# An output projection and a feed-forward's opening as one written sequence, with weights split ahead; a recurrent layer entered before its root

## The chip, the cores and the metric

The kernel runs on one NeuronCore of one Trainium2 chip. The metric is the device time of one execution in microseconds (us), lower is better. Engines are called as the profile calls them: PE is TensorE's matmul, PEld its weight loads, DVE is VectorE, ACT is ScalarE, POOL is GpSimd, SP is SyncE, which here only issues DMAs.

## The reference, cut to what matters

One inference step with two trunk layers over 512 latent and 128 context tokens of width 1024, all in f32. Layer 0 mixes tokens by attention, layer 1 by a gated linear recurrent unit (LRU); each is followed by a SwiGLU feed-forward of inner width 2816. The parts that the change touches:

```python
def _modulate(x, g, shift, scale):            # ahead of each sub-layer
    return _rms_norm(x, g) * (1 + scale[:, None, :]) + shift[:, None, :]

def _swiglu(x, w_gu, w_down):
    gate, up = jnp.split(x @ w_gu, 2, axis=-1)
    return (jax.nn.silu(gate) * up) @ w_down

def _lru_mixer(xm, h0, w_in, conv_w, conv_b, w_a, b_a, w_i, b_i, lam, w_out):
    gate, xr = jnp.split(xm @ w_in, 2, axis=-1)
    xc = _centred_depthwise_conv(xr, conv_w, conv_b).astype(jnp.float32)
    ...                                        # coefficients, two scans: hs_f, hs_b
    y = (hs_f + hs_b).astype(xm.dtype) * jax.nn.gelu(gate)
    return y @ w_out, jnp.stack([hT_f, hT_b], axis=1)

        lat = lat + g1_l[:, None, :] * o_l     # residual behind the mixer
        f_l = _swiglu(_modulate(lat, norm_g[i, 1], sh2_l, sc2_l), ffn_w_gu[i], ffn_w_down[i])
        lat = lat + g2_l[:, None, :] * f_l
```

## The kernel before

Activations lie transposed: features on the 128 partitions (8 tiles of 128, index k or f), the 640 tokens along the free axis. f32 precision comes from splitting every operand into a high part `hi` (a cast to fp32r on ACT, L1217) and a low part `lo` (a difference on DVE, L1218; both in `split`). A product is three matmuls per 128 inputs: hi·hi, hi·lo, lo·hi. `chunk` (L227 and on, matmuls L233 to L235) makes 128 outputs for half of the tokens: 8 × 3 = 24 matmuls of 320 columns. `part` (L242 to L244) does the same for some of the k.

`unit` fetches one weight tile of 1024 × 128 and splits it, or, when its name is in `kept`, loads both parts ready made. `keep` makes these ready parts ahead of time: in the first feed-forward's second and third groups (`ffn`), two units an iteration, POOL loads raw weights into `kraw` (one buffer), ACT casts, DVE subtracts into `kw` (one buffer), POOL stores to DRAM (L197 to L203). Before the change that covers the LRU's 16 input units ("wi") and 8 output units ("wlo").

The order of instructions on each engine is made by a scheduler that works from a model of the durations, except where `in_order` (L1221 and on) fixes it: within its block the instructions of PE, DVE and ACT keep the order of the code. Tiles of a pool lie in memory in the order of their first use, and a pool opened later lies over the memory of those closed before it; a tile there waits for the tiles under it.

The RMS norm's factor per token, the root, is made by `stat` (L449 and on): matmuls of the sum of squares `ssq` and of the last square with a column of ones (L456, "at"), mean plus epsilon on DVE (L459), power −1/2 on POOL (L469), a diagonal matrix on DVE (L471), and a matmul of ones with it that spreads the factor over the partitions (L474, "rr" or "mx"). ACT copies it to `r` (L493 or L860).

The places that the change touches:

- **End of the first feed-forward.** `project` (its down projection) adds residuals (L499), squares, sums `ssq`, and scales x into the LRU's input `hi`, `lo`, without the root. Then `stats` makes the root for both token halves. Only then comes `lru`, in written order on PE, DVE and ACT: per unit f the input half `xa`, `xb`, `e1`, `e2` (L1087, times the root), convolution `c1`, `cv` (L1105, L1109), four gate products (L1118), tanh, exponentials and the scans, and the gate half `ga`, `gb`.
- **Output projection of the LRU.** `project_halves` does three output tiles with both token halves in six banks, with the last input tile last, and then the five others (`DEH`) in two passes over the halves; each residual's x is stored to the DRAM copy `xd` by SP (L836). After each half `stat` makes its root.
- **Opening of the second feed-forward.** `normed`, `first_half` and `second_half` multiply x by gain and root (L804), add the bias on ACT (L805) and split; the blocks are called B11 (first four k, first token half), B21, B12 and B22. `plain` makes hidden units 0 and 1 (`PLAIN` = 2) by ordinary products (L960 to L962). All further hidden units use a seven-product scheme over sums of blocks: `sums` makes T1 to T4 of the blocks (L824 to L827, the last on POOL) and splits them, and reloads x from `xd` for the later residuals; `sum_weights` makes S1 to S4 of the weights (L882) and splits them; `product` (L903 to L905) is called by `pair_a`, `pair_b` and `pair_c`.

Only two short stretches of this projection and opening are in written order before the change; the rest is placed by the scheduler, with `held` to keep some products behind the root's matmuls.

## Time and profile before

| | |
|---|---|
| device time, three executions | 1544.09, 1548.87, 1553.25 us; median 1548.87 |
| profiled execution | 1547.74 us, its span 1546.0 us |
| mean granted clock of TensorE | 0.985 |
| busy share PE / DVE / ACT / POOL | 97% / 70% / 46% / 16% |
| DMA | 238.60 MB moved, 154 GB/s on average |

The span runs from the first to the last instruction; all places in the trace are in us from its start. The first feed-forward's last down projection ends near 855, the LRU runs from there to about 1034, the output projection to about 1077, and the second feed-forward to the end. A line of the trace gives start, duration, engine, code line, operation, written tile and read tiles; "x12" merges twelve in a row, and the bracket is idle time before it with what ended it. A matmul's listed duration overlaps with the next one's, so its cost is the distance of starts. PEclk is the clock that TensorE was granted, as a share of the full one.

### The profile page before, as it was taken

Reading aid. Unit: us, or ns where it says so; the run is one execution under the profiler, and the core shown is the slowest. Engines: PE = TensorE matmul, PEld = TensorE weight load, DVE = VectorE, ACT = ScalarE, POOL = GpSimd, SP = SyncE. Lnnn points to the kernel's source line nnn. Section 1 sums busy time; section 2 is a strip of 40 time slices with the busy share of each in tenths; the row PEclk is TensorE's granted clock in tenths of the full one; section 3 lists DMA queues with packets and bytes.
Section 4 is the critical chain, followed back from the end, with each engine's and each line's share of the span. In section 5 each row is a group of like instructions: output and inputs, shape, how many; then the busy total and the mean of one; then the engine's idle time right before and its main releaser. Section 6 shows DMA issues by size and latency. Waiting matters only on the chain.

```text
span 1546.0 us, 26176 instructions
## 1 busy us (share of the span) xinstructions
PE 1492.1 (97%) x10311; PEld 1446.1 (94%) x10311; DVE 1078.2 (70%) x2040; ACT 713.9 (46%) x1312; POOL 251.6 (16%) x298
## 2 busy tenths in 40 slices
PE   6999999989999999999999999998999999999997
PEld 3899999889999999999999899988999999999997
DVE  5678788969899998555556278884776656565646
ACT  4676666664333123423434377763534343434242
POOL 2111122100111111110110011110132322222210
PEclk9999999999999999999999999999899999999998
DMA  9545556445556668666675533244232231323211
GB/s 378 160 114 167 168 161 183 146 140 192 170 195 187 202 207 276 213 236 229 229 234 175 195 129 123 69 173 161 63 117 82 81 107 58 100 65 99 66 55 68
DMA packets 80011, 238.60 MB, mean 154 GB/s; under 512 B 8816, under 2 KB 24336, under 8 KB 76688
## 3 DMA queue, kind: packets, MB, share of 16 engines
q1 hardware_dynamic: 61136, 157.07, 31.7%
q0 software_dynamic: 18464, 79.71, 16.1%
q8 instruction: 81, 1.33, 0.3%
q14 instruction: 42, 0.34, 0.1%
q10 hardware_dynamic: 288, 0.16, 0.0%
HBM read 196.26 MB, written 34.09 MB: 149 GB/s over the span
## 4 chain that ended last, share of the span: by engine, by line
PE 87%; DVE 6%; DMA 3%; ACT 2%; issue 1%; POOL 0%; SPq 0%; POOLq 0%; DVEq 0%; ACTq 0%
PE mm L233 14%; PE mm L234 14%; PE mm L235 14%; PE mx L235 5%; PE mx L233 5%; PE mx L234 5%; PE mx L903 3%; PE mx L904 3%; PE mx L905 3%; PE gp L1118 2%; PE op L739 2%; PE tp L663 1%; PE mc L903 1%; PE mc L904 1%; PE mc L905 1%; PE mm L257 1%
## 5 line engine op out<-in xcount | busy, mean ns | idle before, releaser
L233 PE MATMUL mm<-big,whi 128*128 128x320 f32 (+3 forms) x1011 | 313.6, 312 | 2.7 <-ACT whi L1217 1.6
L234 PE MATMUL mm<-big,whi 128*128 128x320 f32 (+3 forms) x1011 | 315.0, 312 | 1.2 <-DVE big L1218 1.2
L235 PE MATMUL mm<-big,wlo 128*128 128x320 f32 (+3 forms) x1011 | 314.1, 311 | 0.0
L271 DVE SCALAR_TENSOR_TENSOR mprod<-mraw,csb 128x1024 f32<-128x1024 f32 x160 | 195.5, 1222 | 5.6 <-DMA mraw<-in_wm 5.3
L233 PEld LDWEIGHTS mm<-big,whi 128*128 128x128 f32 x1011 | 190.8, 189 | 4.9 <-ACT whi L1217 1.9
L234 PEld LDWEIGHTS mm<-big,whi 128*128 128x128 f32 x1011 | 191.6, 190 | 2.7 <-DVE big L1218 1.9
L235 PEld LDWEIGHTS mm<-big,wlo 128*128 128x128 f32 x1011 | 191.7, 190 | 1.1
L1217 ACT CAST whi<-raw 128x1024 fp32r<-128x1024 f32 (+2 forms) x110 | 112.6, 1024 | 160.5 <-PE mm L234 105.9
L1218 DVE TENSOR_TENSOR wlo<-raw,whi 128x1024 fp32r<-128x1024 f32 (+2 forms) x110 | 136.3, 1239 | 38.3 <-ACT whi L1217 35.9
L235 PE MATMUL mm<-big,wlx 128*128 128x320 f32 (+3 forms) x498 | 154.7, 311 | 1.9 <-DMA wlx<-kwlo 1.9
L233 PE MATMUL mm<-big,whx 128*128 128x320 f32 (+3 forms) x498 | 154.6, 311 | 0.0
L234 PE MATMUL mm<-big,whx 128*128 128x320 f32 (+3 forms) x498 | 154.6, 310 | 0.0
L499 DVE SCALAR_TENSOR_TENSOR x<-mm,G,x 128x192 f32<-128x192 f32 (+3 forms) x207 | 83.5, 435 | 88.8 <-PE mm L235 88.4
L235 PE MATMUL mx<-big,wlo 128*128 128x320 f32 (+3 forms) x365 | 115.1, 315 | 1.0 <-DMA wlo<-kwlo 1.0
L233 PE MATMUL mx<-big,whi 128*128 128x320 f32 (+3 forms) x365 | 116.0, 318 | 0.0
L234 PE MATMUL mx<-big,whi 128*128 128x320 f32 (+3 forms) x365 | 114.6, 314 | 0.0
L267 POOL DMA_DIRECT2D mraw<-in_wm x80 | 43.2, 540 | 376.5 <-DVE mprod L271 265.3
L235 PEld LDWEIGHTS mm<-big,wlx 128*128 128x128 f32 x498 | 94.2, 189 | 2.1 <-DMA wlx<-kwlo 2.1
L234 PEld LDWEIGHTS mm<-big,whx 128*128 128x128 f32 x498 | 94.3, 189 | 0.0
L233 PEld LDWEIGHTS mm<-big,whx 128*128 128x128 f32 x498 | 94.1, 189 | 0.0
L1217 ACT CAST whx<-raw 128x1024 fp32r<-128x1024 f32 (+1 forms) x38 | 39.0, 1026 | 73.3 <-PE mm L234 42.2
L235 PEld LDWEIGHTS mx<-big,wlo 128*128 128x128 f32 x365 | 70.4, 193 | 1.5 <-DMA wlo<-kwlo 1.5
(332 smaller groups left out, 3719.7 us busy)
## 6 DMA issues: line engine op xcount, KB each, us to landing
raw<-in_gu SPq DMA_DIRECT2D x88, 512.0 KB, 3.6
mraw<-in_wm POOLq DMA_DIRECT2D x80, 512.0 KB, 3.9
kwi<-kw POOLq DMA_DIRECT2D x16, 1024.0 KB, 5.2
raw<-in_dn SPq DMA_DIRECT2D x24, 512.0 KB, 3.6
sw<-in_wm SPq DMA_DIRECT2D x16, 512.0 KB, 10.1
raw<-in_wqk SPq DMA_DIRECT2D x16, 512.0 KB, 4.4
kraw<-in_wi POOLq DMA_DIRECT2D x16, 512.0 KB, 6.1
kwlo<-kw POOLq DMA_DIRECT2D x8, 1024.0 KB, 5.2
```

The costliest lines, as they stand in the source:

```text
L233: nc.tensor.matmul(ps, hi[:, k], xhi[:, k, s], start=(k == 0), stop=False)
L234: nc.tensor.matmul(ps, hi[:, k], xlo[:, k, s], start=False, stop=False)
L235: nc.tensor.matmul(ps, lo[:, k], xhi[:, k, s], start=False, stop=(k == nk - 1))
L267: nc.gpsimd.dma_start(w, self.i["wm"][l * 6 + j - 2, f])
L271: nc.vector.scalar_tensor_tensor(prod, w, 1.0, self.csb[:, s], ALU.mult, ALU.mult, accum_out=out[:, s, f:f + 1])
L499: last = self.nc.vector.scalar_tensor_tensor(xs, ps[:, a - t0:b - t0], G[:, s, f:f + 1], xs, ALU.mult, ALU.add).ins
L739: mm = nc.tensor.matmul(out, v, w, start=start, stop=stop)
L903: nc.tensor.matmul(ps, hi[:, k], xh[:, k], start=start and k == 0, stop=False, skip_group_check=not start)
L904: nc.tensor.matmul(ps, hi[:, k], xl[:, k], start=False, stop=False, skip_group_check=not start)
L905: nc.tensor.matmul(ps, lo[:, k], xh[:, k], start=False, stop=(k == KH - 1), skip_group_check=not start)
L1217: self.nc.scalar.copy(hi, v)
L1218: return self.nc.vector.tensor_tensor(lo, v, hi.bitcast(F32), ALU.subtract).ins
```

## The change

It makes four edits.

1. `keep` also splits five units of the second feed-forward's gate and up weights (gate and up of hidden units 0 and 1, and the gate of unit 2), three units instead of two in each group's last iteration.
2. `stat` is cut into `root`, `diag` and `spread`. At the end of the first feed-forward `stats` is replaced by `entry`: seven eighths of the LRU's first product, then the root's matmuls over all 640 tokens at once (the last square is added to `ssq` on DVE), then the last eighth. The diagonal, the product of the other token half, the spread and the copies follow in `whole`, a new step of the LRU's written order.
3. `project_halves`, `plain` and the first lines of `ffn_halves` become one function, `opening`, wholly in written order on PE, DVE and ACT. In it `xd` is stored by POOL instead of SP, all weights of units 0 and 1 come ready split, T4 is made on DVE, the first S1 to S4 stand at fixed places, and x is reloaded after the weights of six units are asked for. The second root's and first root's matmuls, diagonal and spread stand inside other chunks.
4. The weight tiles of the opening's pool are first used ahead of the others, and the LRU's gate tile `gl` ahead of its input tiles, so the memory order of both pools is another.

The diff, cut to its core:

```diff
-            nc.gpsimd.dma_start(raw, self.i[name][f])
+            nc.gpsimd.dma_start(raw, self.i[name][1, f] if name == "gu" else self.i[name][f])
...
-        if k < KT - 1:
+        if k < KT - 1 or self.whole:
             nc.vector.tensor_tensor(self.ssq[:, s], self.ssq[:, s], q, ALU.add)
         self.lastq[t0] = [q]
...
+    def root(self, bl, parts, newton=False):
+        nc, n = self.nc, len(bl)
         ps = self.ps()
-        parts = [(self.ssq, 0)] + [(q, t0) for q in self.lastq.get(t0, ())]
...
+    def entry(self, hi, lo):
+        self.u0, self.p0 = self.unit(("wi", KT), "m"), self.pg(False)
+        t0, t1 = CHB[0]
+        ps = self.p0[:, 0:t1 - t0]
+        with self.in_order(ORDERED[:1]):
+            self.part(ps, self.u0, hi, lo, range(KT - 1), t0, t1)
+            self.rs = self.root(range(0, NTOK, P), [(self.ssq, 0)])
+            self.part(ps, self.u0, hi, lo, (KT - 1,), t0, t1)
...
-        if nxt:
+        if entry:
+            self.shift(*nxt)
+            self.entry(*nxt[1:])
+        elif nxt:
             self.stats()
             self.shift(*nxt)
...
         todo = [("wi", KT), ("wi", 0)] + [("wi", f + g) for f in range(1, KT) for g in (KT, 0)] + [("wlo", f) for f in range(KT)]
+        todo += [("gu", c * NF + f) for f in range(PLAIN) for c in range(2)] + [("gu", PLAIN)]
...
                 if ci:
-                    self.keep(todo, 2)
+                    self.keep(todo, 3 if j == n - 1 else 2)
...
+    def opening(self, w, hi, lo, gk, key, xd, l):
+        nc = self.nc
+        G = self.need(self.gcols, gk)
+        us = [self.unit(w[f], "m" if f < KT - DEH else "x") for f in range(KT - 2)]
+        self.load_x(xd)
+        banks = [(f, c, (self.ps("mx") if c else self.pg(False))[:, 0:HT]) for f in range(KT - DEH) for c in range(2)]
+        self.ssq = self.t([P, NTOK], F32, "ssq", 1, self.sb)
+        self.lastq, qs, hid, tmp = {}, {}, {}, {}
+
+        def mm(f, c, ks=range(KT), ps=None):
+            ps = self.pg()[:, 0:HT] if ps is None else ps
+            self.part(ps, us[f], hi, lo, ks, *CH[c])
+            return ps
+
+        def res(f, c, ps):
+            t0, t1 = CH[c]
+            self.residual(f, t0, t1, ps, G, False)
+            qs[f, c] = q = self.ssq[:, t0:t1] if f == 0 else self.t([P, HT], F32, "sq", 2, self.sb)
+            nc.scalar.activation(q, self.x[:, f, t0:t1], AF.Square)
+            nc.gpsimd.dma_start(xd[f * P:f * P + P, t0:t1], self.x[:, f, t0:t1])
+            if f == KT - 1:
+                self.lastq[t0] = [q]
+
+        def add(f, c):
+            t0, t1 = CH[c]
+            if 0 < f < KT - 1:
+                nc.vector.tensor_tensor(self.ssq[:, t0:t1], self.ssq[:, t0:t1], qs[f, c], ALU.add)
+
+        def start(s):
+            self.stat_spread(s)
+            nc.scalar.copy(self.rt[:, s[0]:s[1]], self.r[0][:, 0:s[1] - s[0]])
+
+        def halves(k, c):
+            n = f"B{1 + k // KH}{1 + c}"
+            return [self.X[n + p][:, k % KH] for p in "hl"]
+
+        def gain(k, c):
+            for s, a, b in _pieces(*CH[c]):
+                v = self.x[:, k, a:b]
+                nc.vector.scalar_tensor_tensor(v, v, A[:, s, k:k + 1], self.rt[:, a:b], ALU.mult, ALU.mult)
+            for s, a, b in _pieces(*CH[c]):
+                v = self.x[:, k, a:b]
+                nc.scalar.activation(v, v, AF.Identity, bias=B[:, s, k:k + 1])
+            nc.scalar.copy(halves(k, c)[0], self.x[:, k, slice(*CH[c])])
+
+        def low(k, c):
+            h, v = halves(k, c)
+            nc.vector.tensor_tensor(v, self.x[:, k, slice(*CH[c])], h.bitcast(F32), ALU.subtract)
+
+        def plain(u, c, ks=range(KT), ps=None):
+            ps = self.pg(False)[:, 0:HT] if ps is None else ps
+            for k in ks:
+                xh, xl = halves(k, c)
+                nc.tensor.matmul(ps, u[0][:, k], xh, start=(k == 0), stop=False)
+                nc.tensor.matmul(ps, u[0][:, k], xl, start=False, stop=False)
+                nc.tensor.matmul(ps, u[1][:, k], xh, start=False, stop=(k == KT - 1))
+            return ps
+
+        def gate(j, ps):
+            hid[j] = self.t([P, HT], F32, "g", 3, self.sb)
+            nc.scalar.activation(hid[j], ps, AF.Silu)
+
+        def outs(j, c):
+            return [t[:, j, c * HT:c * HT + HT] for t in (self.hhi, self.hlo)]
+
+        def up(j, c, ps):
+            nc.vector.tensor_tensor(hid[j], ps, hid[j], ALU.mult)
+            nc.scalar.copy(outs(j, c)[0], hid[j])
+
+        def rest(j, c):
+            nc.vector.tensor_tensor(outs(j, c)[1], hid[j], outs(j, c)[0].bitcast(F32), ALU.subtract)
+
+        def sums(k):
+            b11, b12, b21, b22 = [self.x[:, j, a:a + HT] for j in (k, k + KH) for a in (0, HT)]
+            t2 = self.t([P, HT], F32, "c22", 2, self.sb)
+            tmp[k] = ("T1", b11), ("T2", t2), ("T3", b12), ("T4", b21)
+            for n, v in zip(("T1", "T2", "T3", "T4"), ((b11, b12, b11), (t2, b22, b11), (b12, b22, b12), (b21, b21, t2))):
+                nc.vector.tensor_tensor(*v, ALU.subtract)
+                nc.scalar.copy(self.X[n + "h"][:, k], v[0])
+
+        def lows(k):
+            for n, v in tmp[k]:
+                nc.vector.tensor_tensor(self.X[n + "l"][:, k], v, self.X[n + "h"][:, k].bitcast(F32), ALU.subtract)
+            for j in (k, k + KH):
+                nc.sync.dma_start(self.x[:, j], xd[j * P:j * P + P])
+
+        last = KT - 1
+        self.blocks(self.t([P, 2 * KH, HT], F32R, "xt", 1, self.sb), ("T4h", "T4l"))
+        with self.in_order():
+            for ks in (range(KT - 2), (KT - 2,), (KT - 1,)):
+                for f, c, ps in banks:
+                    mm(f, c, ks, ps)
+            us += [self.unit(w[f], "m") for f in (KT - 2, KT - 1)]
+            f = KT - DEH
+            ps = mm(f, 0)
+            for i, (g, c, bank) in enumerate(banks):
+                res(g, c, bank)
+                if i:
+                    add(*banks[i - 1][:2])
+            res(f, 0, ps)
+            add(*banks[-1][:2])
+            add(f, 0)
+            for f in range(f + 1, KT):
+                res(f, 0, mm(f, 0))
+                add(f, 0)
+            f = KT - DEH
+            ps = mm(f, 1, range(KH))
+            st = self.stat_root(*CH[0])
+            mm(f, 1, range(KH, KT), ps)
+            st = self.stat_diag(st)
+            res(f, 1, ps)
+            add(f, 1)
+            f += 1
+            ps = mm(f, 1, range(KH))
+            start(st)
+            mm(f, 1, range(KH, KT), ps)
+            gain(0, 0)
+            gain(1, 0)
+            self.hhi, self.hlo = [self.big(n=NTOK + 2) for _ in range(2)]
+            for t, n in ((self.hhi, "T2"), (self.hlo, "T3")):
+                self.blocks(t, (n + "h", n + "l"))
+                h = t.rearrange("p k t -> p (k t)")[:, 2 * (NTOK + 2):2 * (NTOK + 2) + HB]
+                self.X["B12h" if n == "T2" else "B12l"] = h.rearrange("p (k t) -> p k t", k=KH)
+            self.hhi, self.hlo = [t[:, :, 0:NTOK] for t in (self.hhi, self.hlo)]
+            g0 = self.unit(("gu", 0), "m")
+            u0 = self.unit(("gu", NF), "x")
+            raw = self.t([P, KT, P], F32, "raw", 3)
+            nc.sync.dma_start(raw, self.i["gu"][l, PLAIN])
+            q = {"g": raw, "u": self.i["gu"][l, NF + PLAIN]}
+            for f in range(f, last):
+                k = 2 * (f - KT + DEH)
+                res(f, 1, ps)
+                ps = mm(f + 1, 1)
+                gain(k, 0)
+                low(k - 2, 0)
+                gain(k + 1, 0)
+                low(k - 1, 0)
+                add(f, 1)
+            low(KT - 2, 0)
+            low(KT - 1, 0)
+            res(last, 1, ps)
+            g1, u1 = self.unit(("gu", 1), "m"), self.unit(("gu", NF + 1), "m")
+            hi2, lo2 = self.unit(("gu", PLAIN), "x")
+            q["W"] = {n: (hi2[:, a:a + KH], lo2[:, a:a + KH]) for n, a in (("A11", 0), ("A12", KH))}
+            ps = plain(g0, 0, range(KH))
+            st = self.stat_root(*CH[1])
+            plain(g0, 0, range(KH, KT), ps)
+            gate(0, ps)
+            s12, s34 = self.s_sums(q)
+            s12(True)
+            st = self.stat_diag(st)
+            s34(True)
+            self.s_split(q, 0)
+            ps = plain(u0, 0, range(KH))
+            start(st)
+            plain(u0, 0, range(KH, KT), ps)
+            gain(0, 1)
+            up(0, 0, ps)
+            gate(1, plain(g1, 0))
+            gain(1, 1)
+            low(0, 1)
+            rest(0, 0)
+            for k in range(2, 6):
+                gain(k, 1)
+                low(k - 1, 1)
+            ps = plain(u1, 0)
+            up(1, 0, ps)
+            gain(6, 1)
+            low(5, 1)
+            rest(1, 0)
+            self.pair_a(q, False)
+            gain(7, 1)
+            low(6, 1)
+            low(7, 1)
+            sums(0)
+            q["g1"] = self.total(*q["g1"], "g")
+            lows(0)
+            sums(1)
+            gate(0, plain(g0, 1))
+            lows(1)
+            ps = plain(u0, 1)
+            sums(2)
+            up(0, 1, ps)
+            lows(2)
+            rest(0, 1)
+            gate(1, plain(g1, 1))
+            sums(3)
+            self.s_split(q, 1)
+            lows(3)
+            self.last_weights(q)
+            up(1, 1, plain(u1, 1))
+            rest(1, 1)
+        return q
...
+    def s_sums(self, q):
+        nc, g = self.nc, q["g"]
         q["u"], src = self.t([P, KT, P], F32, "raw", 3), q["u"]
         nc.sync.dma_start(q["u"], src)
+        ss = q["S"] = [self.t([P, KT, P], F32, "sum", 2, self.sb) for _ in range(2)]
         s1, s2, s3, s4 = [s[:, a:a + KH] for s in ss for a in (0, KH)]
         g1, g2, u1, u2 = [t[:, a:a + KH] for t in (g, q["u"]) for a in (0, KH)]
+        ops = (s1, u1, u2, ALU.add), (s2, s1, g1, ALU.subtract), (s3, g1, u1, ALU.subtract), (s4, g2, s2, ALU.subtract)
+
+        def run(two):
+            def go(vector):
+                for o in two:
+                    (nc.vector if vector else nc.gpsimd).tensor_tensor(*o)
+            return go
+        return run(ops[:2]), run(ops[2:])
+
...
         def xa(f, z):
-            z["u"] = self.unit(("wi", KT + f), "m")
+            z["u"] = self.unit(("wi", KT + f), "m") if f else self.u0
             z["gw"] = tile([P, 2, 2, P], "gw", 2)
             nc.sync.dma_start(z["gw"], self.i["wg"][f])
-            z["ps"] = self.chunk(z["u"], hi, lo, *CHB[0], ps=self.ps("mx"))
+            z["ps"] = self.chunk(z["u"], hi, lo, *CHB[0], ps=self.ps("mx")) if f else self.p0[:, 0:CHB[0][1] - CHB[0][0]]
             z["b"] = bias(z["ps"], CHB[0][0])
 
+        def whole(f, z):
+            if f == 0:
+                dg = tile([P, NT, P], "gl", 3)
+                self.diag(dg, self.rs, NT)
+                z["pb"] = self.chunk(z["u"], hi, lo, *CHB[1], False)
+                ps = self.pp.tile([P, 1024], F32, tag="gp", name=self.nm("gp"), bufs=2)
+                self.spread(dg, range(0, NTOK, P), ps, 0)
+                self.rt = self.t([P, NTOK], F32, "r", 1)
+                for _, a, b in _pieces(0, NTOK):
+                    nc.scalar.copy(self.rt[:, a:b], ps[:, a:b])
+
         def xb(f, z):
-            z["pb"] = self.chunk(z["u"], hi, lo, *CHB[1], False)
+            if f:
+                z["pb"] = self.chunk(z["u"], hi, lo, *CHB[1], False)
...
         def ga(f, z):
+            z["g"] = tile([P, NTOK], "gl", 3)
             z["v"] = self.unit(("wi", f), "x")
             z["pg"] = self.chunk(z["v"], hi, lo, *CHB[0], False)
-            z["g"] = tile([P, NTOK], "gl", 3)
...
+        order = ((g[0], 0), (h[0], 0), (g[1], 0), (h[1], 0), (cl, 0), (e[0], 0), (e[1], 0), (g[2], 0), (xa, 1), (whole, 1), (g[3], 0), (d[0], 0),
...
-        self.load_x(xd)
-            self.blocks(self.t([P, 2 * KH, HT], F32R, "xt", 1, fp), ("T4h", "T4l"))
-            self.project_halves([("wlo", f) for f in range(KT)], yhi, ylo, (1, 2), (1, 1), xd)
...
-            self.ffn_halves(1, (1, 1), xd)
+            q = self.opening([("wlo", f) for f in range(KT)], yhi, ylo, (1, 2), (1, 1), xd, 1)
+            self.ffn_halves(1, q)
```

178 lines of the change are left out of this document (48 added, 130 removed).

## The prediction

> **What bounds it now.** I read the page's head first, then the busy table in stretches of 10 us, then the table of waits between the two places that the diff touches, and last the timelines there.
>
> ```profile
> span 1546.0 us, 26176 instructions
> PE 1492.1 (97%) x10311; PEld 1446.1 (94%) x10311; DVE 1078.2 (70%) x2040; ACT 713.9 (46%) x1312; POOL 251.6 (16%) x298
> ```
>
> ```profile
> core 0: us, PE busy (x) PEld busy (x) DVE busy (x) ACT busy (x) POOL busy (x), PEclk, DMA share, GB/s
> 850.00:860.00 10.00, 8.22 (x63) 8.13 (x61) 4.60 (x13) 3.10 (x8) 1.43 (x2) 1.00 0.65 198
> 860.00:870.00 10.00, 9.11 (x45) 8.85 (x46) 1.39 (x5) 1.50 (x7) 0.28 (x1) 0.66 0.90 308
> 1070.00:1080.00 10.00, 7.69 (x54) 7.43 (x52) 9.13 (x22) 8.97 (x20) 0.00 (x0) 1.00 0.15 44
> 1080.00:1090.00 10.00, 4.61 (x20) 4.64 (x21) 5.96 (x11) 3.35 (x7) 0.85 (x1) 0.63 0.33 112
> 1130.00:1140.00 10.00, 7.27 (x40) 6.75 (x39) 5.67 (x8) 4.80 (x8) 0.02 (x1) 0.86 0.52 158
> 1150.00:1250.00 100.00, 100.00 (x684) 100.00 (x683) 63.35 (x107) 37.73 (x61) 26.11 (x21) 1.00 0.27 79
> ```
>
> ```profile
> PE at L456 <- DVE ssq L445: 7.7, 1, 7.7
> PE mx L903 <- ACT snap L909: 2.7, 1, 2.7
> PE mm L235 <- DMA wlx<-kwlo: 1.9, 1, 1.9
> PE mx L235 <- DMA wlo<-kwlo: 1.0, 1, 1.0
> ```
>
> TensorE bounds the kernel: 97% busy, and in ordinary stretches 684 matmuls start in 100 us, 0.146 us each, 3.50 us for a chunk of 24. Only the gaps can be won. The busy table shows them around 850 to 870 (entry of the recurrent layer) and 1070 to 1140 (output projection and opening of the second feed-forward), each with a lowered clock right behind. The waits name what ended last in the second place. Time saved there should reach the end, since TensorE is full from 1150 on.
>
> **Entry of the recurrent layer.** Now two roots (24 narrow passes, two powers, two diagonals, 12 spreading passes) stand between the last projection and the first LRU chunk.
>
> ```profile
> 855.48 1.40 PE L456 MATMUL at<-ones,ssq 128*128 128x1 f32 x12
> 856.74 1.48 PE L456 MATMUL at<-ones,sq 128*128 128x1 f32 x12
> 855.69 0.68 DVE L499 SCALAR_TENSOR_TENSOR x<-mx,G,x 128x192 f32<-128x192 f32 x2 [0.93 <-PE mx L235]
> 863.63 0.43 ACT L493 COPY r<-rr 128x320 f32<-128x320 f32 x1 [1.99 <-PE rr L474]
> 869.21 0.63 DVE L1087 TENSOR_TENSOR xr<-mx,r 128x192 f32<-128x192 f32 x2 [7.39 <-ACT bias L1066]
> 872.57 0.75 DVE L1087 TENSOR_TENSOR xr<-mm,r 128x64 f32<-128x64 f32 x2 [2.53 <-PE mm L235]
> 873.40 1.20 ACT L1105 ACTIVATE xc<-xr,cbs,cols 128x512 f32<-128x512 f32 x2 [3.71 <-issue]
> 874.64 2.74 DVE L1109 SCALAR_TENSOR_TENSOR xc<-xr,cols,xc 128x643 f32<-128x643 f32 x3 [1.32 <-ACT xc L1105]
> 879.64 3.38 PE gp L1118 x12
> 1069.70 0.68 PE mx L474 x6
> 859.11 0.32 SPq L187 DMA_DIRECT2D whx<-kwi  x1
> whx<-kwi SPq DMA_DIRECT2D x4, 512.0 KB, 5.1
> ```
>
> After the change TensorE does, from 855.48: 21 matmuls of the first unit (3.07), one root of 10 passes (24 passes took 2.74, so 1.14), 3 matmuls (0.44), 24 (3.50), 10 spreading passes (6 took 0.68, so 1.13), the gate unit's 48 (7.01): 16.3 us, the gates at 871.8. The vector side from the spread's end at 864.8: two copies 0.86, products 0.63 and 0.75, bias and three taps 1.20 and 2.74, about 0.4 for small steps: 871.4. TensorE is later, so the gates come 879.64 − 871.8 = **7.8 us** earlier. The root's input has its cover: the last residual ends at 856.37, square and the added sum some 1.7 later, 858.1, against TensorE's 858.55. The power and the wider diagonal, about 2.1, lie under 27 matmuls (3.94); without that cover they cost it all.
>
> Two things take from this. The gate weights leave at 859.11 and 0.4 later and land 5.1 after, 864.2 and 864.6, where they are wanted at 864.8; with the extra traffic below I take 1.0 (0 to 3). The other is that traffic: five more units (gate and up of units 0 and 1, gate of unit 2) are split ahead of time in the first feed-forward.
>
> ```profile
> L201 DVE TENSOR_TENSOR kw<-kraw,kw x24: 1215/1225/1227, 578.6 to 813.3; 128x1024 fp32r<-128x1024 f32 x24
> L203 POOL DMA_DIRECT2D kwi<-kw x16: 538/538/538, 580.4 to 734.7; - x16
> L203 POOL DMA_DIRECT2D kwlo<-kw x8: 538/538/547, 746.7 to 814.8; - x8
> ```
>
> These stores run as a chain, load, cast, difference, store, through one buffer: 24 between 580.4 and 814.8 is one per 10.2 us, whatever number an iteration may ask for. Five more end at 814.8 + 51 = 866, not under the projection's 855 but across the new entry. Inside the projection a cast and 1.22 us of DVE per 10 us cost nothing (DVE is 46% busy in 850:860; the banks absorb the rest). Across the entry they cost between 0 and a whole period; I take 1.5, since each engine there is mostly idle. Entry: 7.8 − 1.0 − 1.5 = **5.3 us**, bounds 0 and 7.8.
>
> **Projection and opening.** Removed: the two weight waits, 2.9 (units 3 to 5 go to slots that lie over memory the LRU frees earlier); the 7.7 us for the sum of squares, since ACT and DVE now take squares and sums in written order, ahead of work that can wait; and the 2.7 us at L903, a DVE and ACT backlog: five raw splits of 1.2 us on DVE and 1.05 on ACT leave. The clock goes with them.
>
> ```profile
> 1085.39 1.41 PE L456 MATMUL at<-ones,ssq 128*128 128x1 f32 x6 [7.70 <-DVE ssq L445]
> 1087.94 0.61 PE L960 MATMUL mm<-big,whi 128*128 128x320 f32 x1
> 1088.89 0.47 PE L960 MATMUL mm<-big,whi 128*128 128x320 f32 x1
> 1089.16 0.47 PE L961 MATMUL mm<-big,whi 128*128 128x320 f32 x1
> 1095.23 4.83 DVE L804 SCALAR_TENSOR_TENSOR x<-x,A,r 128x192 f32<-128x192 f32 x16 [5.43 <-ACT r L860]
> 1095.69 1.10 ACT L805 ACTIVATE x<-x,B 128x192 f32<-128x192 f32 x3 [0.49 <-DVE x L804]
> 1104.60 1.69 DVE L1218 TENSOR_TENSOR big<-x,big 128x320 fp32r<-128x320 f32 x4
> 1106.47 1.06 ACT L1217 CAST whx<-sum 128x1024 fp32r<-128x1024 f32 x1
> 1111.81 1.21 DVE L1218 TENSOR_TENSOR wlx<-sum,whx 128x1024 fp32r<-128x1024 f32 x1
> 1125.80 1.58 DVE L1218 TENSOR_TENSOR xt<-x,xt 128x320 fp32r<-128x320 f32 x1
> 1125.48 1.54 POOL L882 TENSOR_TENSOR sum<-raw,raw 128x512 f32<-128x512 f32 x1
> x<-xd SPq DMA_DIRECT2D x4, 640.0 KB, 5.8
> ```
>
> After the long wait 12 passes took 2.55 instead of 1.37, and matmuls start 0.27 apart, 0.12 too late each, for 18 of them until about 1093: 1.2 + 2.2. Behind the L903 wait 13 did: 1.6. Removed in all: 2.9 + 7.7 + 3.4 + 2.7 + 1.6 = 18.3.
>
> Added is strict order on TensorE, DVE and ACT. Let T0 be the end of the projection's last chunk. TensorE then needs eight plain chunks, pair_a, a root and a spread: 9 × 3.50 + 1.37 + 0.68 = 33.5, and wants the last part of T2 at 34.9. On ACT the silu of unit 1 stands ahead of the second gain and waits for its chunk: 3.50 + 1.37 + 3.50 + 0.68 + 3.50 = 12.6, done at 12.9. Behind it come seven gains at about 1.2 (0.60 on DVE, two biases 0.66 and a cast 0.35 on ACT, each engine waiting in turn for the other), and a snapshot: 21.8, the last low part 22.3; the plain chunk that reads it gets there at 22.6, just behind. Then DVE does 31 operations of 0.40 (four sums, three sets of lows, total, product, rest): 34.8. ACT casts S3/S4 (1.06, from 35.2), DVE splits them (1.14) and writes two more lows: 38.2. TensorE waits 3.3 at T2, which at the clock that followed 2.7 costs another 1.6. Splits of the next unit's gate weights that fall between: 1.2, one DVE split (0 to 5). The stores of x go from SP to POOL, 16 issues of 0.54, of which the one power behind them sees none, its own data coming later; they free SP. The reload of x for the residuals now lies over gate tiles that the LRU's last unit holds until its last product, and stands on SP behind six weight loads; I take 0.5 (0 to 5.8, its landing time, less if TensorE still has free banks). Net 18.3 − 3.3 − 1.6 − 1.2 − 0.5 = **11.7 us**, bounds 3 and 18.3.
>
> The Trainium skill (TensorE: Matmul & The Clock Gate, Why this matters for your kernels) warns of a lower clock only beyond idle gaps of about 3 us. The trace lowered it behind waits of 2.7 and, at the entry, of 2 us at most amid narrow passes; by the page alone the 1.6 would stay open and the forecast could be 1.6 lower.
>
> **Sum.** The profiled execution took 1547.74 (span 1546.0), 1.1 below the median 1548.87. 5.3 + 11.7 = 17.0, so 1530.7 against it, **1532** against the median. All bounds at their best give 26, 1523; a difference below 0.5% (7.7 us) I count as no change, about what a measurement here can tell.
>
> **Rivals.** *POOL collides with DVE* (0.17). POOL's four sums for unit 3 were held behind the last T4 difference; now only the second root's power holds them, so they may fall into the chain of 31 operations. Beside POOL's 1.54 a DVE operation of 0.40 took 1.58: in 6 us DVE does 4 or 5 instead of 14, losing 4.2. The wait at T2 becomes 7.5: 1536. Against it: they need their raw weights, which need a buffer. The Trainium skill (GPSIMD Engine Reference, Key points) says that POOL shares its SBUF interfaces with VectorE and contends with DVE instructions of two SBUF inputs; the two rows agree.
>
> *The entry wins nothing* (0.14). The root's power queues on POOL behind a store of the late chain, and that store waits for DVE until 866: spread at 869 instead of 863.6, 5.4 more and about 2 of slow clock. Entry 0, total 11.7: 1537. For it: the dates coincide. Against: the power is ready first.
>
> *Slower* (0.11). The late casts and differences stand on ACT and DVE ahead of the projection's last residuals and wait there for their loads. Four free banks of 21 matmuls cover some 12 us, so nothing shows until the last residual; from there TensorE idles until the chain ends. At 10.2 a unit that is some 10 us, a total still below before; if the period grows to 15 beside the LRU's weight loads (DMA at 0.90 in 860:870), the chain ends at 890, TensorE idles 34 less the 7.8 gained, and the time is 1549 − 12 + 26 = 1563. It decides from a period of about 13. The last kept store's date tells it.
>
> **Chances.** Forecast 0.58 (its own range 1523 to 1540), rivals 0.17, 0.14, 0.11. Below 1541: 0.55 + 0.12 + 0.08 = 0.75; within 0.5%: 0.15; slower 0.10, nearly all from the third rival. The range 1520 to 1546 leaves that rival and the tails out.
>
> **What would show it.** Right: gates about 7 us after the spread and 16 after the projection; no narrow passes idle for 7 us; no DMA wait in the projection; a wait of 2 to 5 us at the first T2 product. Wrong: kept stores past 870, waits of ACT on kraw near 855, POOL sums beside the T lows, or new gaps in the full stretch after 1150.

## Result, and the profile after

| | before | after |
|---|---|---|
| device time, median | 1550.62 us (four runs, 1544.09 to 1553.25) | 1534.01 us (four runs, 1532.30 to 1535.37) |
| ratio after / before | | 0.9899, 95% interval 0.9864 to 0.9933 |
| profiled execution, its span | 1547.74, 1546.0 us | 1532.30, 1530.5 us |

The change is faster by 1.0%, and 1532 was forecast. The sum came out; several of its terms did not, as the last parts show. Three landmarks show it, the starts of single instructions in the two profiles: the last residual of the first feed-forward, the first gate product of the LRU, the last gate product. The views of one tile, here the residual's and the gate's, give first and last start of each group of instructions. Before:

```profile
L499 DVE SCALAR_TENSOR_TENSOR x<-mx,G,x x4: 341/381/420, 849.5 to 856.0; 128x192 f32<-128x192 f32 x2, 128x128 f32<-128x128 f32 x2
```

```profile
L1118 PE MATMUL gp<-xc,gw x16: 274/432/697, 879.5 to 887.4; 128*128 128x512 f32 x8, 128*128 128x131 f32 x8
```

After:

```profile
L527 DVE SCALAR_TENSOR_TENSOR x<-mx,G,x x2: 342/376/411, 850.7 to 851.0; 128x192 f32<-128x192 f32 x1, 128x128 f32<-128x128 f32 x1
```

```profile
L1273 PE MATMUL gp<-xc,gw x16: 274/432/697, 879.6 to 887.5; 128*128 128x512 f32 x8, 128*128 128x131 f32 x8
```

| stretch of the profiled execution | before | after | difference |
|---|---|---|---|
| start to the last residual | 856.0 | 851.0 | −5.0 |
| from there to the first gate product ("entry") | 23.5 | 28.6 | +5.1 |
| first to last gate product | 137.3 | 137.3 | 0 |
| from there to the last matmul ("end stretch") | 522.3 | 506.3 | −16.0 |

So the entry, forecast to win 5.3, lost 5.1; projection and opening, forecast to win 11.7, won 16.0; and 5.0 lie ahead of both, where TensorE's instructions stand in the same order in both kernels up to 805. Most of those 5.0 go with the granted clock, which differs from execution to execution there. The busy table in stretches of 10 us (columns as in the prediction), before and then after:

```profile
170.00:180.00 10.00, 9.84 (x72) 8.77 (x72) 7.41 (x20) 4.75 (x10) 0.57 (x1) 0.83 0.44 119
380.00:390.00 10.00, 10.00 (x64) 10.00 (x63) 6.66 (x15) 2.39 (x6) 2.81 (x3) 0.81 0.38 111
```

```profile
170.00:180.00 10.00, 10.00 (x87) 9.37 (x86) 7.90 (x22) 5.14 (x12) 0.57 (x1) 1.00 0.53 152
380.00:390.00 10.00, 10.00 (x77) 10.00 (x76) 7.38 (x17) 1.48 (x3) 3.76 (x4) 1.00 0.46 135
```

Fifteen and 13 matmuls fewer at 0.15 us each are 4.2 us. In the fourteen profiles of this study the last residual starts between 849.1 and 856.8, so a median of four runs can carry some us that are no edit's; below, entry and end stretch are what is compared. The last 367 matmuls of the end stretch, which no edit touches, vary too: 59.1 us before, 58.1 after, 57.3 to 60.4 in the fourteen profiles, at granted clocks of 1.00 to 0.94. So 1.0 of the 16.0 is theirs. By entry and end stretch the change is worth 10.9 us in this pair.

The busy table after, at the places that the prediction showed:

```profile
core 0: us, PE busy (x) PEld busy (x) DVE busy (x) ACT busy (x) POOL busy (x), PEclk, DMA share, GB/s
850.00:860.00 10.00, 8.30 (x59) 8.03 (x57) 4.51 (x10) 2.21 (x5) 2.63 (x4) 1.00 0.71 245
860.00:870.00 10.00, 2.26 (x12) 1.69 (x12) 4.14 (x9) 2.33 (x8) 0.22 (x1) 0.57 0.97 355
870.00:880.00 10.00, 9.30 (x47) 9.08 (x48) 0.49 (x1) 0.16 (x1) 0.00 (x0) 0.74 0.50 203
1070.00:1080.00 10.00, 10.00 (x73) 10.00 (x72) 7.01 (x19) 6.17 (x12) 2.30 (x4) 1.00 0.72 241
1080.00:1090.00 10.00, 10.00 (x72) 10.00 (x71) 8.75 (x14) 4.91 (x12) 3.21 (x3) 1.00 0.27 90
...
1110.00:1120.00 10.00, 8.97 (x58) 8.20 (x56) 8.49 (x14) 5.84 (x10) 2.96 (x2) 1.00 0.26 75
```

1080 to 1090 was 4.61 busy at clock 0.63 and is full. 860 to 870 was 9.11 busy and is 2.26: twelve matmuls in 10 us, with the DMA engines at 0.97. TensorE's waits after, first in 840 to 900, then in 1000 to 1160 (us in total, times, longest):

```profile
PE mm L233 <- DMA whx<-kwi: 7.2, 1, 7.2
PE gp L474 <- DVE gl L470: 1.9, 1, 1.9
PE mm L235 <- DMA wlx<-kwi: 1.0, 1, 1.0
```

```profile
PE mx L242 <- ACT lt L1283: 2.6, 1, 2.6
PE mx L1078 <- ACT snap L1084: 1.1, 2, 0.6
PE mm L233 <- DVE x L527: 1.0, 1, 1.0
PE mx L1079 <- DVE big L917: 0.5, 1, 0.5
```

Behind the spread TensorE waits 8.2 us for the first gate unit's weights. SP's timeline says why, and below it the DMA issues at 859.63 (the last number is the time from issue to landing):

```profile
851.35 0.32 SPq L1471 DMA_DIRECT2D xd<-x  x1
858.19 0.32 SPq L187 DMA_DIRECT2D whi<-kwi  x1
858.60 0.38 SPq L187 DMA_DIRECT2D wlo<-kwi  x1
859.03 0.42 SPq L1215 DMA_DIRECT2D gw<-in_wg  x1
859.63 0.33 SPq L187 DMA_DIRECT2D whx<-kwi  x1
```

```profile
kgu<-kw POOLq DMA_DIRECT2D x1, 1024.0 KB, 10.3
whx<-kwi SPq DMA_DIRECT2D x1, 512.0 KB, 9.1
```

The narrow units are the input halves ("wi", KT + f); they share three slots `whi`, `wlo`, while the gate halves lie in `whx`, `wlx`. `whi`, `wlo` at 858.19 are the fourth narrow unit, wanted three units later. Its slot is that of the first unit, whose last product starts at 857.99; SP stood on it from 851.7, then sent its 1 MB ahead of `whx`. The last kept store, another 1 MB, left POOL at 859.62, together with `whx`. In the kernel before, `whx` left at 859.11 with 4.2 to landing; here it took 9.1, and the store 10.3.

### The profile page after: what moved, and what is told of

The parts are those of the page before. It is cut to its first block, busy times and chain, and to the rows that moved or that the text cites. A ratio compares the mean times of both kernels' runs of the same rounds, so it can differ in the third digit from the quotient of the medians.

```text
span 1530.5 us, 26161 instructions
## 1 busy us (share of the span) xinstructions
PE 1478.7 (97%) x10295; PEld 1433.8 (94%) x10295; DVE 1075.5 (70%) x2044; ACT 716.9 (47%) x1312; POOL 261.7 (17%) x319
## 3 DMA queue, kind: packets, MB, share of 16 engines
q0 software_dynamic: 20672, 90.20, 17.9%
## 4 chain that ended last, share of the span: by engine, by line
PE 88%; DVE 4%; DMA 3%; ACT 2%; issue 1%; POOL 1%; SPq 0%; DVEq 0%; POOLq 0%; ACTq 0%
PE mm L233 13%; PE mm L235 13%; PE mm L234 13%; PE mx L233 5%; PE mx L235 5%; PE mx L234 5%; PE mx L1078 3%; PE mx L1079 3%; PE mx L1080 3%; PE gp L1273 2%; PE op L772 2%; PE tp L696 1%; PE mc L1078 1%; PE mc L1080 1%; PE mc L1079 1%; PE mm L257 1%
## 5 line engine op out<-in xcount | busy, mean ns | idle before, releaser
L234 PE MATMUL mm<-big,whi 128*128 128x320 f32 (+3 forms) x995 | 308.8, 311 | 1.7 <-DVE big L1373 1.6
L233 PE MATMUL mm<-big,whi 128*128 128x320 f32 (+3 forms) x995 | 307.9, 311 | 2.4 <-DVE x L527 1.2
L235 PE MATMUL mm<-big,wlo 128*128 128x320 f32 (+3 forms) x995 | 307.9, 310 | 0.3 <-DVE wlo L1373 0.3
L233 PEld LDWEIGHTS mm<-big,whi 128*128 128x128 f32 x995 | 186.7, 188 | 4.9 <-ACT big L1372 2.1
L234 PEld LDWEIGHTS mm<-big,whi 128*128 128x128 f32 x995 | 187.5, 189 | 3.1 <-DVE big L1373 2.2
L233 PE MATMUL mm<-big,whx 128*128 128x320 f32 (+3 forms) x466 | 145.5, 312 | 7.2 <-DMA whx<-kwi 7.2
L235 PE MATMUL mm<-big,wlx 128*128 128x320 f32 (+3 forms) x466 | 145.5, 312 | 1.0 <-DMA wlx<-kwi 1.0
L234 PE MATMUL mm<-big,whx 128*128 128x320 f32 (+3 forms) x466 | 145.4, 312 | 0.0
L527 DVE SCALAR_TENSOR_TENSOR x<-mm,G,x 128x192 f32<-128x192 f32 (+3 forms) x207 | 83.3, 436 | 73.8 <-PE mm L235 64.0
L233 PE MATMUL mx<-big,whi 128*128 128x320 f32 (+2 forms) x325 | 101.6, 313 | 0.0
L234 PE MATMUL mx<-big,whi 128*128 128x320 f32 (+2 forms) x325 | 100.8, 310 | 0.0
L235 PE MATMUL mx<-big,wlo 128*128 128x320 f32 (+2 forms) x325 | 100.8, 310 | 0.0
L233 PEld LDWEIGHTS mm<-big,whx 128*128 128x128 f32 x466 | 88.7, 190 | 7.4 <-DMA whx<-kwi 7.4
L235 PEld LDWEIGHTS mm<-big,wlx 128*128 128x128 f32 x466 | 88.7, 190 | 1.4 <-DMA wlx<-kwi 1.4
L234 PEld LDWEIGHTS mm<-big,whx 128*128 128x128 f32 x466 | 88.8, 191 | 0.0
L235 PE MATMUL mx<-big,wlx 128*128 128x320 f32 (+3 forms) x222 | 69.0, 311 | 0.0
```

Source lines behind the costliest of these rows:

```text
L233: nc.tensor.matmul(ps, hi[:, k], xhi[:, k, s], start=(k == 0), stop=False)
L234: nc.tensor.matmul(ps, hi[:, k], xlo[:, k, s], start=False, stop=False)
L235: nc.tensor.matmul(ps, lo[:, k], xhi[:, k, s], start=False, stop=(k == nk - 1))
L527: last = self.nc.vector.scalar_tensor_tensor(xs, ps[:, a - t0:b - t0], G[:, s, f:f + 1], xs, ALU.mult, ALU.add).ins
```

## The experiments

Two theories for the entry: **A**, SP's order puts a load that can wait ahead of the gate weights; **B**, the kept stores of the five added units reach into the entry. For the opening: **O**, written order, or **P**, presplit weights. Medians are of four runs or more; ratios to the kernel before with 95% intervals. (The expectations of x1 to x3 count the entry 0.3 longer: 28.9 and 23.8 for 28.6 and 23.5.)

| run | entry | end stretch | median us | ratio |
|---|---|---|---|---|
| before | 23.5 | 522.3 | 1550.6, 1547 to 1549 beside the runs below | |
| after | 28.6 | 506.3 | 1534.0 | 0.9899 (0.9864 to 0.9933) |
| x1 SP order | 21.7 | 507.5 | 1529.6 | 0.9879 (0.9858 to 0.9900) |
| x2 early gate | 19.7 | 519.1 | 1536.7 | 0.9931 (0.9909 to 0.9952) |
| x3 no last keep | 18.6 | 506.7 | 1525.9 | 0.9857 (0.9838 to 0.9877) |
| x4 narrow bank | 29.6 | 505.7 | 1532.2 | 0.9901 (0.9877 to 0.9925) |
| x5 entry only | 15.9 | 526.5 | 1541.4 | 0.9963 (0.9948 to 0.9977) |
| x6 opening only | 24.0 | 515.1 | 1541.7 | 0.9959 (0.9943 to 0.9975) |
| x7 presplit only | 26.0 | 522.8 | 1548.4 | 1.0003 (0.9992 to 1.0015) |
| x8 order only | 15.9 | 514.3 | 1531.6 | 0.9883 (0.9858 to 0.9908) |
| x9 early gate, layout | 19.8 | 505.4 | 1527.5 | 0.9859 (0.9820 to 0.9899) |
| x10 opening, layout | 24.5 | 504.3 | 1531.8 | 0.9892 (0.9865 to 0.9918) |
| x11 earlier keeps | 15.9 | 506.2 | 1523.6 | 0.9844 (0.9820 to 0.9868) |
| x12 earlier keeps, bank | 15.9 | 506.1 | 1518.8 | 0.9814 (0.9789 to 0.9840) |

### x1: the order on SP alone

```diff
         def xa(f, z):
-            z["u"] = self.unit(("wi", KT + f), "m") if f else self.u0
+            with self.tc.issue_after(self.gate0) if f == 3 else nullcontext():   # gate0: the first gate unit's load
+                z["u"] = self.unit(("wi", KT + f), "m") if f else self.u0
```

> The changed kernel with the load of the recurrent layer's fourth narrow unit held behind the first gate unit's load on SP. In the changed kernel SP stands on that fourth unit's slot until 858.2 and then sends its 1 MB ahead of the first gate unit's weights, for which TensorE waits 7.2 + 1.0 us; the last residual is 28.9 us ahead of the first gate product (23.8 before the change). Theory A (order on SP): the gate weights leave about 1.5 us earlier and with 1 MB less in front of them, which at 355 GB/s is 2.8 us; the wait falls to about 4 us, the distance to 24 to 25, the time by 4 us to 1530. Rival B (the late kept stores: the last of them, 1 MB, leaves at 859.6 beside the gate weights, and its cast and difference stand ahead of the diagonal): the wait stays above 6 and the time within 1.5 us of the changed kernel's 1534.

The wait for the gate weights fell from 8.2 to 1.0, the entry from 28.6 to 21.7. TensorE's waits in 840 to 900, and two rows of SP's timeline:

```profile
PE gp L474 <- DVE gl L470: 1.8, 1, 1.8
PE mm L235 <- DMA wlx<-kwi: 0.7, 1, 0.7
PE mm L233 <- DMA whx<-kwi: 0.3, 1, 0.3
```

```profile
862.19 0.32 SPq L187 DMA_DIRECT2D whx<-kwi  x1
...
865.77 0.59 SPq L187 DMA_DIRECT2D whi<-kwi  x1
```

A holds, by more than expected; the kept stores all stay, so B alone is out. `whx` now also leaves ahead of the last store (864.26) and lands in 4.3. So 6.9 of the entry's loss is what SP's order costs beside that store; no run has this order without the store.

### x2 and x9: the first gate unit loaded during the projection

```diff
         self.u0, self.p0 = self.unit(("wi", KT), "m"), self.pg(False)
+        self.v0 = self.unit(("wi", 0), "m")
...
-            z["v"] = self.unit(("wi", f), "x")
+            z["v"] = self.unit(("wi", f), "x") if f else self.v0
```

> The changed kernel with the first gate unit's presplit weights loaded during the projection, into a slot of the narrow units that belongs to the outer pool. Theories A and B alike: no wait for DMA behind the spread; the 48 gate matmuls run from 861.3 to 868.4 at full clock, the convolution's last tap ends at 867.7, so the gate products come 18 to 19 us after the last residual instead of 28.9; the time falls by about 10 us, to 1524. Rival C (something else in the entry sets the gates: vector work, the recurrence's steady period, or the wait for the convolution): the distance falls by less than 5, or the gain is gone again before the layer ends, and the time stays above 1530.

The entry is 19.7, close to the expectation, but the gain is gone again, as rival C allows: the median is 1536.7 against 1534.0, and the end stretch grew by 12.8, of which 2.3 are the last 367 matmuls. Waits in 1015 to 1060, and SP's first weight load for the projection:

```profile
PE mm L242 <- DVE x L528: 7.2, 1, 7.2
PE mx L242 <- ACT lt L1284: 2.6, 1, 2.6
```

```profile
1028.99 0.32 SPq L187 DMA_DIRECT2D whx<-kwlo  x1
```

That is 17.0 behind the last gate product; in the changed kernel it left at 1022.40, 5.5 behind. Tiles lie in the order of their first request. The layer's weight slots are now first requested by its second unit, behind the vector tiles `lt`; these moved down from 189216 to 164640 (bytes in a partition), under the next phase's first weight slot at 162912, and SP holds all loads behind it until the layer's last operation on them. x9 requests every tile of the layer, and its narrow bank, once in the old order, writing nothing:

```diff
+        self.ps("mx")
+        tile([P, 2, 2, P], "gw", 2)
+        tile([P, NTOK], "gl", 3)
+        tile([P, 648], "xr", 2)
...
+        for n in ("whx", "wlx"):
+            self.t([P, KT, P], F32R, n, self.wx, lp)
...
```

> The early gate weights again, with the recurrent layer's tiles and its narrow bank requested once, unused, ahead of the layer, so that memory and banks lie where they lay: the narrow bank is bank 3, and the gate weights' slots come ahead of the vector tiles. Without that (x2) the vector tiles moved to 164640 and up, under the first weight slots of the next phase, and SP sent the projection's weights at 1029.0 instead of 1022.4. Theory (layout): the 7.2 us wait for x in the projection and the 2.6 us wait for a bank both go; from the last gate product to the end 504 to 506 us instead of 519.1; entry 19 to 20 us as before; time 1521 to 1524. Rival (the early load itself delays the projection): 514 or more and 1530 or more.

The end stretch is 505.4. Up to its last 367 matmuls it is 11.7 shorter than in x2: the tiles' place had cost 10.5, and 1.2 more are won with the bank in its old place. The entry is 19.8, as in x2; the median is 3 us above the expectation, with a last residual at 856.8, 5.8 later than in the changed kernel's profile.

### x3: without the last kept unit

```diff
-        todo += [...] + [("gu", PLAIN)]
+        todo += [...]
...
-            hi2, lo2 = self.unit(("gu", PLAIN), "x")
+            hi2, lo2 = [self.t([P, KT, P], F32R, n, 3, self.sb) for n in ("whx", "wlx")]
+            self.split(hi2, lo2, raw)
```

> The changed kernel without the last of the 29 kept units (gate weights of unit 2), which the opening splits from raw weights instead. Its cast (857.0), difference (858.1 to 859.3) and 1 MB store (859.6) no longer fall into the entry. Theory A (order on SP): the diagonal comes about 1.9 us earlier, but SP still sends the fourth unit first; without the store the first gate weights land about 2 us earlier; the distance from the last residual to the gate products falls from 28.9 to about 26.5, and the split (1.05 on ACT, 1.2 on DVE) costs 0 to 1 in the opening: 1532 to 1533. Rival B (the kept stores): the wait for the gate weights nearly goes, distance 22 or less, time 1527 or less.

The numbers are those of B (18.6; 1525.9), but the run does not tell the two apart: with one unit less the scheduler itself moved the fourth narrow unit behind the gate weights (864.35 against 860.68 on SP). Against x1, which has that order and the last unit, the last unit costs 3.1 at the entry. The end stretch is 0.4 longer than in the changed kernel, less than the 1.5 that a lower clock behind the bank's wait took here (last section), so its raw split shows no cost.

### x4: the narrow bank requested first

```diff
         Z = [{} for _ in range(KT)]
+        self.ps("mx")
```

> The changed kernel with the recurrent layer's bank for narrow products requested ahead of its gate banks, as it was before the change; nothing else. In the changed kernel the gate pair's banks are 3 to 6 and the narrow bank is 7 (before: 3, and 4 to 7), so the projection's second bank is one that the layer's last tanh still reads, and TensorE waits 2.6 us for it at 1017. Theory (banks): that wait goes and the time falls by 2.6 us, to 1531.4. Rival (the wait only moves to the next bank or to the last unit's vector chain): the projection's third or later bank waits instead, and the time stays within 1 us.

The narrow bank (`mx`) takes the first products of the input halves. The 2.6 us wait is gone, and with it 2.1 up to the 3000th matmul of the end stretch; two waits of 0.45 and 0.56 follow in the projection, the second of them for x (L527). The last 367 matmuls, which the bank doesn't touch, took 59.6 instead of 58.1, so 0.6 is left at the end. The cause of the wait is shown; what it is worth is taken up in x12. (The entry's 29.6 has a wait of 9.3 for the gate weights in it.)

### x5 and x6: each half alone

x5 is the new entry with the old projection and opening and 24 kept units; x6 the reverse:

```diff
-                             lambda f: nc.sync.dma_start(xd[f * P:f * P + P], self.x[:, f]), entry=True)
+                             lambda f: nc.sync.dma_start(xd[f * P:f * P + P], self.x[:, f]))
...
-            z["u"] = self.unit(("wi", KT + f), "m") if f else self.u0
+            z["u"] = self.unit(("wi", KT + f), "m")
```

> The kernel before with the new entry of the recurrent layer alone: old projection and opening, 24 kept units, none in the entry. Measured so far from the last residual to the first gate product: 23.5 us before, 28.6 after, 21.7 with SP's order mended, 18.6 without the last kept unit. Theory (the entry is good, and what spoilt it were the late kept stores and the order on SP that came with them): 17 to 19 us, so 5 to 6 us won there; 2 to 3 us are given back at the layer's end, where the narrow bank has moved to bank 7; the time falls by 2 to 4 us, to about 1544. Rival (the new entry itself does not shorten the chain): 22 us or more, and the time stays or rises by the 2.6 us at the end.

The view of the gate's tile in x5:

```profile
L1163 PE MATMUL gp<-xc,gw x16: 274/432/697, 871.8 to 879.8; 128*128 128x512 f32 x8, 128*128 128x131 f32 x8
```

The last residual starts at 855.9, so the entry is 15.9: the new form wins 7.5 where no kept unit is late. The end stretch gives back 4.2: the moved bank's 2.6 and a new 4.7 us wait for the projection's weights, which SP sends 17.9 behind the last gate product, against a shorter wait of the second root (3.5).

> The changed kernel with the old entry of the recurrent layer: two roots ahead of the first unit. Written opening and 29 kept units stay. Theory: the opening carries the whole gain. From the layer's last gate product to the last matmul 522.3 us before and 506.3 after with a 2.6 us wait for a bank in it; here that wait is absent (the narrow bank is bank 3 again), so about 504; the entry stays at 23.5 us or up to 3 more through the late kept stores; the time is 1528 to 1532, below the changed kernel's 1534. Rival (the two halves need each other): the entry grows beyond 27 us, or the end stretch stays at 506, and the time is 1534 or more.

The entry is 24.0 as expected, the end stretch is not: 515.1. TensorE's longest wait there, and SP's first weight load:

```profile
PE mx L242 <- issue: 9.6, 1, 9.6
```

```profile
1032.69 0.32 SPq L187 DMA_DIRECT2D whx<-kwlo  x1
```

That is 15.4 behind the last gate product. It is x2's mechanism: the new entry is the first to ask for the gate's tile `gl`, for its diagonal, so `gl` lies at 146528; without it `gl` lies at 156960 to 164640, again under 162912, and is read by the layer's last product on DVE. The view names no releaser of the 9.6 us; DVE's timeline does:

```profile
1045.51 0.55 DVE L527 SCALAR_TENSOR_TENSOR x<-mm,G,x 128x320 f32<-128x320 f32 x1 [11.22 <-DMA x<-xd]
```

TensorE has its first weights, but no free bank: the residuals that empty the banks wait for the reload of x, which stands on SP behind the six weight loads. The 7.2 us in x2 (`x L528`) are the same wait.

### x10: the opening alone, with `gl` requested first

```diff
+        tile([P, 2, 2, P], "gw", 2)
+        tile([P, NTOK], "gl", 3)
```

> The opening alone again (x6), with the tile that the new entry is the first to request, the gate's, requested once ahead of the layer, so that it lies at 146528 as in the changed kernel and not at 156960 to 164640, under the next phase's first weight slot at 162912. In x6 SP sent the projection's weights at 1032.7, behind the layer's last product, instead of 1022.4, and TensorE stood 9.6 us. Theory (layout): that wait goes; from the last gate product to the end 503 to 506 us instead of 515.1, the entry stays at 24, the time falls by about 10 to 1531 or 1532. Rival (the written opening needs the new entry's timing): 510 or more and 1538 or more.

```profile
1020.43 0.32 SPq L187 DMA_DIRECT2D whx<-kwlo  x1
```

It leaves 5.6 behind the last gate product, as in the changed kernel. The end stretch is 504.3, so the two unused requests are worth 10.8. The opening alone wins 18.0 (16.1 without the last 367 matmuls), and 10.8 of that hang on where one tile of the previous layer lies.

### x7 and x8: presplit weights or written order alone

```diff
 # x7, on the kernel before
-        us = [[self.unit(self.i["gu"][l, c * NF + f]) for c in range(2)] for f in range(PLAIN)]
+        us = [[self.unit(("gu", c * NF + f)) for c in range(2)] for f in range(PLAIN)]
...
 # x8, on the changed kernel
-            g0 = self.unit(("gu", 0), "m")
+            g0 = self.unit(self.i["gu"][l, 0], "m")
...
```

> The kernel before with the five units of the second feed-forward split ahead of time (29 kept units), with the old entry and the old opening in the order that the planner gives. Theory O (the 7.7 us wait of the second root came from the planner's order of work on DVE and ACT): a wait of 5 us or more ahead of that root stays, and the stretch from the layer's last gate product to the last matmul falls from 522.3 by 3 to 6, the waits for weights and for the fifth splits alone. Rival P (it came from the five raw splits, 1.2 us on DVE and 1.05 on ACT each, in the queue ahead of squares and sums): the wait falls below 3 and the stretch by 10 or more.

Waits of x7 in 1005 to 1180:

```profile
PE at L456 <- DVE ssq L445: 4.4, 1, 4.4
PE mx L907 <- ACT snap L913: 3.9, 1, 3.9
PE mx L235 <- DMA wlo<-kwlo: 2.3, 2, 1.9
PE mm L235 <- DMA wlx<-kwlo: 1.3, 1, 1.3
PE mx L233 <- DMA whi<-kwlo: 1.0, 1, 1.0
```

The root's wait shrank from 7.7 to 4.4, the one for a snapshot grew from 2.7 to 3.9 and those for weights from 2.9 to 4.6, and nothing was won: 522.8.

> The changed kernel with the five units of the opening split from raw weights where they are written (24 kept units). Theory O (written order): no wait ahead of the second root; the five splits cost 5.3 us of ACT and 6 of DVE that strict order puts in line, of which up to 5 show ahead of the T products; from the layer's last gate product to the last matmul 507 to 512 us (506.3 after, 522.3 before). Rival P (presplitting): 515 or more, with waits of 5 us and more in 1050 to 1130. The late kept stores are gone too, so the entry should take 17 to 19 us as without the last kept unit.

514.3, between the two expectations: order alone wins 8.0 with the bank's wait in it, and the presplit units, worth nothing alone, win another 8.0 on top (7.4 and 7.6 without the last 367 matmuls). In x8 the casts and differences stand in line ahead of the second root (timeline, then the busy table):

```profile
1070.67 0.83 PE L453 MATMUL at<-ones,ssq 128*128 128x1 f32 x6 [0.54 <-DVE ssq L860]
1072.66 1.44 PE L453 MATMUL at<-ones,sq 128*128 128x1 f32 x6 [1.16 <-ACT sq L852]
```

```profile
1070.00:1080.00 10.00, 8.29 (x37) 8.04 (x36) 7.21 (x13) 6.11 (x10) 1.42 (x2) 0.66 0.40 132
```

Two waits of 1.7 together, and then a lower clock: 37 matmuls in 10 us where the changed kernel does 73. The entry, without late stores, is 15.9.

### x11 and x12: the kept units started earlier

```diff
-                if ci:
+                if ci or j > 4:
                     self.keep(todo, 3 if j == n - 1 else 2)
```

> The changed kernel with the split ahead of time started three units of the first feed-forward earlier, beside the modulations, so that the 29 kept units end before the entry; nothing is left out. Theory (the late kept stores, and SP's order that came with them, spoil the entry, nothing else): last store at about 810 to 825, entry 15.9 us as in the two kernels without late stores, end stretch 506: 12.7 us less than the changed kernel, 1521. Rival (DVE, busy 98% of 520 to 550, has no room there): gaps on TensorE or a later end of the modulations before 600, of 5 us or more, and 1527 or more.

The last store leaves at 791.7, earlier than expected, the scheduler puts the gate weights first by itself, and the first of them land in 3.8 instead of 9.1. The view of the gate's tile, the DMA issue of those weights, and the busy table of the stretch that takes the earlier units:

```profile
L1273 PE MATMUL gp<-xc,gw x16: 274/432/697, 871.6 to 879.5; 128*128 128x512 f32 x8, 128*128 128x131 f32 x8
```

```profile
whx<-kwi SPq DMA_DIRECT2D x1, 512.0 KB, 3.8
```

```profile
440.00:600.00 160.00, 160.00 (x1085) 160.00 (x1084) 145.24 (x256) 49.78 (x83) 26.39 (x50) 1.00 0.79 270
```

Entry 15.9, 12.7 less than after, and TensorE has no gap in 440 to 600, although DVE is 91% busy there. The median is 2.6 above the expectation; its last residual starts at 855.6, 4.7 later than in the changed kernel's profile.

x12 adds x4's line:

> The earlier kept units together with the narrow bank requested first; the version put together from these experiments. The bank alone won 2 us of the 2.6 us wait in the trace. Theory (the two add): entry 15.9, end stretch 503.5 to 504.5, time 1518 to 1520. Rival (the freed time is given back at the layer's end, where the last unit's vector chain is next): the end stretch stays at 506 and the time within 1 us of the kernel with the earlier keeps alone.

The rival came true. TensorE no longer waits for the bank, but then for the reload of x:

```profile
PE mm L242 <- DVE x L527: 1.6, 1, 1.6
```

The end stretch is 506.1, as without the line. x12's median is 4.8 below x11's, but its last residual starts at 849.1 against 855.6, so in these two profiles the lower time lies ahead of what x12's line touches; in 380 to 390 the granted clock was 1.00 in x12 and 0.81 in x11. All runs of x11 (1523.2 to 1524.1) and x12 (1517.7 to 1521.2) lie below all of the changed kernel's; that the bank adds anything is not shown.

## Why the prediction was right, and where it was wrong

- **Entry, 5.3 (0 to 7.8): wrong, +5.1.** The form of the entry was sized rightly: 7.8 forecast, 7.5 in x5, x8 and x11. The term "gate weights 1.0 (0 to 3)" failed: 8.2 of waiting and a low clock behind it. I took issue time and landing from the row of the kernel before and moved the consumer, but not the queue: the first narrow unit now frees its slot late, SP asks for that slot before the gate weights, and what it then sends stands in front of them. The scheduler chose that order only with all five units late; with the same entry in x3, x5, x8, x11 and x12 the gate weights go first. x1 prices the order at 6.9; x1 to x9, 1.9 more for what was left of the weights' wait; x9 to x11, 3.9 for the late kept unit on ACT and DVE, where I had taken 1.5: in x9 its difference on DVE (864.76) stands ahead of the diagonal, for which TensorE waits 3.6. Together 12.7.
- **The late chain, 10.2 a unit, ending at 866: right in its date.** The last store left at 859.6, 5.0 earlier like all else in that execution; beside the gate weights it then took 10.3 to land. The third rival (a period over 13) did not come.
- **Second rival, the entry wins nothing: right that nothing was won (5.1 were lost), wrong in mechanism.** The power ran on POOL at 855.88, ahead of the store.
- **Removed, 18.3: the waits named are gone,** the 7.7 us one, those for weights, the 2.7 us one and the lowered clock behind them. But the end of the weight waits was put down to the opening's slots; x6 and x10 show that the loads leave in time only with `gl` where the entry's request moved it. The two edits are not independent.
- **Added, 6.6: too much.** x10 wins 18.0, or 16.1 without the last 367 matmuls, where 11.7 net was forecast. The waits at the T products are 1.6, not 3.3, and the clock stayed at 1.00 in 1110 to 1120 (1.6 forecast). The reload of x (0.5, 0 to 5.8) costs nothing that shows in this run, but 7.2 in x2, 9.6 in x6 and 1.6 in x12: it depends on when SP gets to it. A 1.0 us wait at 1143.9, for a residual that stands behind a split on DVE, was not forecast.
- **Not foreseen: the 2.6 us wait for the projection's second bank.** The entry's spread asks for the gate banks first, so they moved from 4 to 7 to banks 3 to 6 and the narrow one from 3 to 7; the projection then meets a bank that the last tanh reads. x4 removes the wait; the reload of x takes its place in x12.
- **First rival, POOL beside DVE: it came, but small.** Two of POOL's sums fell beside two of the last low parts, which took 1.59 and 1.56 instead of 0.49. The waits at the T products, with this in them, total 1.6. One pair, from the timeline after:

```profile
1115.03 1.48 POOL L1051 TENSOR_TENSOR sum<-raw,raw 128x512 f32<-128x512 f32 x1 [26.29 <-DVE wlx L1373]
1115.27 1.59 DVE L917 TENSOR_TENSOR big<-c,big 128x320 fp32r<-128x320 f32 x1
```

- **The sum.** 17.0 was forecast and 15.5 came in the spans, by −5.0 ahead of the change, +5.1, −16.0 and +0.5 behind the last matmul (each rounded). The entry came 10.4 worse than forecast and the end stretch 4.3 better; the 5.0 of another granted clock, which no edit made, fill most of the gap. That the total agrees so closely is luck; the parts say more.

## What to carry to other kernels

When a step moves earlier, move its loads with it on paper: read in what order the issuing queue sends them, what that queue stands on, and whether a load that can wait goes first. Where memory and banks are given out by first request, any reordering also moves tiles and changes which transfer waits for whom; compare the addresses before and after, and request tiles once, unused, in the order that is wanted. Work split ahead of time has a due date as well: start it early enough that its last store lands before the next latency-bound stretch.
